# A fifth Strassen pair in two branches of a gated-mixer layer, with the weight sums made in place

## The chip, the cores and the metric

One core of a Trainium2 chip runs the whole layer. The metric is device time in microseconds (us). Names of engines as the profile has them: PE is TensorE (matmuls), PEld its weight loads, DVE is VectorE, ACT is ScalarE, POOL is GpSimd, SP is SyncE, whose queue issues most loads from HBM.

## What is computed

One layer on 256 rows of 2048 channels. An input projection `x @ w_in` gives the inputs of three mixers (a: gated linear recurrence, b: windowed attention, c: short convolution) and three gate inputs `m_a`, `m_b`, `m_c`. Each mixer's output is projected back to 2048 channels, the three are merged by sigmoid gates, projected once more, and layer-normalised. Cut to what matters here:

```python
u = x @ w_in[l]
(..., m_a, m_b, m_c) = jnp.split(u, split_idx, axis=-1)        # 2048 columns each
o_a = o_a * rsqrt(mean(o_a**2, -1) + RMS_EPS)                  # per head of 128
o_a = o_a.reshape(bsz, t, HGRN_WIDTH) * hgrn_norm_g[l]         # one weight per channel
y_a = (o_a * silu(a_g)) @ w_proj_hgrn[l]
y_b = (o_b * silu(b_g)) @ w_proj_attn[l]
y_c = (o_c * silu(c_g)) @ w_proj_conv[l]
merged = sigmoid(m_a) * y_a + sigmoid(m_b) * y_b + sigmoid(m_c) * y_c
x = layer_norm(ALPHA * x + merged @ w_out[l])
```

Everything is float32. The matmuls run on rounded operands (fp32r): each operand is split into a high part `hi` (a cast on ACT) and a low part `lo` (a subtraction on DVE), and a product is three matmuls, hi·hi + lo·hi + hi·lo.

## The kernel before

**Stages.** The time up to 526 us goes to the input projection of the mixers (functions `rows512`, `columns256`, both through `gemm`), with the mixers themselves run as generators (`hgrn`, `attn`, `sums_of_x`) that `pump()` advances a step at a time. Then come the three branches. Each branch has two halves, and a half is one *gate group* (`pair_of_groups`, which computes 1024 gate columns of `x @ w_in`) and two projections of 512 columns (`gemm(a[wp][d], outs[br], NC, "rows")`, 48 matmuls each). After the branches `gemm(a["w_out"][2], ...)`, one more `pair_of_groups` on the first 1024 columns of `w_out`, and the last 512 columns with the layer norm.

**A gate group.** Its 2048 rows of weights come as eight *pairs* of 128-row blocks, one load of 1 MB each into a `raw` buffer (pool `rawp`, three buffers). `PAIRS` says which pairs go by Strassen's scheme. An ordinary pair is two halves of 128x1024 weights: a cast to `hi` on ACT, a subtraction to `lo` on DVE, twelve matmuls, and so 24 matmuls for the pair. A Strassen pair needs seven products, 21 matmuls. Besides `hi`/`lo` of three raw blocks (128x1024 and 128x512, lines 705 to 708) it needs four sums of weights: three subtractions on DVE write them into a tile `w` (lines 702 to 704, straight from `raw`), one cast on ACT gives `hw` (128x2048), and one subtraction on DVE gives `lw` (128x2048, line 712). Before, pairs 1, 3, 5 and 7 are Strassen pairs in all seven groups, and each group opens with an ordinary pair. The matching sums of x (`sums`) are made once by `sums_of_x`; those of the merged rows (`msums`) by `turn`.

**What sets the order.** The kernel is written in order, and a scheduler interleaves the instructions when the program is built; on the chip each engine then runs its own list strictly in order. A list waits at an instruction until the tiles that it reads are written and the buffer that it writes is free. `hi` has four buffers, `lo` four, `raw` three; `hw` and `lw` are single buffers in pool `mgp`, with a second one from pool `w8` for every other Strassen pair (`spare`). A `raw` buffer is loaded again (SP's queue, line 688) once its last reader is done.

**Lines that the steps touch.** L114/L115: cast to hi, hw and subtraction to lo, lw. L702 to L704: sums of weights. L677 to L679: the matmuls of a gate group. L143 to L145: those of a projection. L191: copies of finished accumulators on ACT. L596: the norm weights of mixer a, multiplied into its gate on POOL. L766 to L769: four loads of 1 MB (x, and the layer norm's weights) issued from ACT's queue near the end.

Of the kernel before, what the change touches and what calls it, by code (L numbers as in the profile page):

```python
# [50 lines left out]
def hybrid_kernel(ctx, tc, a, out):  # L51
# [501 lines left out]
    def sums_of_x():  # L553

        n = len(pairs)
        xr = rawp.tile([P, n, 2, T], F32, tag="raw", name="xr")
        for i, p in enumerate(pairs):
            nc.sync.dma_start(out=xr[:, i], in_=a["xT"][:, 2 * p : 2 * p + 2])
        sx = t8([P, 4, n, P], "sx")
        block_sums([sx[:, j] for j in range(4)], xr[:, :, 0, :P], xr[:, :, 1, :P], xr[:, :, 0, P:], xr[:, :, 1, P:])  # L560
        yield
        for i in range(0, n, 2):
            dst = t8([P, 2, 4, 2, P], "sums", F32R)
            sums.append(dst)
            for j in range(2):
                split_to(dst[:, j], sx[:, :, i + j])
            yield
# [81 lines left out]
    msums = []  # L649

    def turn(m, d):
        dst = t8([P, 4, 2, T], "m", F32R)
# [275 lines left out]
```

## Time and profile before

| | us |
|---|---|
| median of 3 runs | 1004.09 (1003.54 to 1006.46) |
| the profiled execution | 1005.54 |
| its span, first to last instruction | 1003.6 |
| PE busy | 985.9 (98%) |
| PE weight loads busy | 833.0 (83%) |
| DVE busy | 808.5 (81%) |
| ACT busy | 562.7 (56%) |
| POOL busy | 33.0 (3%) |

The span is the stretch that the trace covers; the 1.9 us between it and the execution's own time lie around it. Busy shares are averages over the stages. What matters is whether the list of one engine ever stands still for another, and how far ahead of PE the casts and subtractions run.

### The profile page before, as it was taken

How to read it: one execution, taken by the hardware profiler on the slowest of the kernel's cores; microseconds unless marked ns; L12 is line 12 of the kernel's file. 1: busy time of each engine (PE TensorE's matmuls, PEld its weight loads, DVE VectorE, ACT ScalarE, POOL GpSimd, SP SyncE). 2: the span in 40 equal slices, each digit the busy share in tenths (PEclk: the TensorE clock that was granted, in tenths of full speed). 3: DMA queues.
4: the chain of work that ended last, by engine and by line, in shares of the span. 5: the costliest groups of instructions: out<-in, count | busy, mean ns of one | idle time of the engine just before them, and what ended most of it. 6: DMA issues, size and time to landing. Idle time of an engine off the chain costs nothing.

```text
span 1003.6 us, 13714 instructions
## 1 busy us (share of the span) xinstructions
PE 985.9 (98%) x5418; PEld 833.0 (83%) x5418; DVE 808.5 (81%) x1022; ACT 562.7 (56%) x735; POOL 33.0 (3%) x32
## 2 busy tenths in 40 slices
PE   8999999999999999999999999999999999999995
PEld 5888888888888888888888888888888888888884
DVE  6557889689965667768778898897989889897997
ACT  5545668557564655645655555555555555564551
POOL 1000100220010000000000000000000000000003
PEclk9999999999999999999999999999999999999998
DMA  8745545444455446544455655555556556548542
GB/s 315 262 172 206 173 163 171 166 171 169 169 182 196 174 162 196 182 169 166 174 200 178 220 198 206 210 205 194 216 183 210 209 195 215 180 169 336 205 167 84
DMA packets 30831, 193.67 MB, mean 193 GB/s; under 512 B 3840, under 2 KB 4640, under 8 KB 8752
## 3 DMA queue, kind: packets, MB, share of 16 engines
q1 hardware_dynamic: 28944, 185.90, 52.2%
q10 hardware_dynamic: 1152, 4.72, 1.2%
q0 software_dynamic: 672, 2.20, 0.8%
q8 instruction: 42, 0.69, 0.3%
q14 instruction: 21, 0.17, 0.0%
HBM read 190.68 MB, written 2.12 MB: 192 GB/s over the span
## 4 chain that ended last, share of the span: by engine, by line
PE 92%; DVE 5%; DMA 1%; issue 1%; ACT 1%; SPq 0%; DVEq 0%; ACTq 0%
PE acc L151 24%; PE acc L150 11%; PE acc L143 9%; PE p L677 9%; PE acc L145 9%; PE p L679 9%; PE p L678 9%; PE acc L144 9%; DVE lo L115 1%; PE acc L153 1%; PE sc L464 1%; PE pvb L507 1%; DMA raw<-in_w_rows 1%; DVE xres L799 1%; PE pT L497 1%
## 5 line engine op out<-in xcount | busy, mean ns | idle before, releaser
L114 ACT CAST hi<-raw 128x1024 fp32r<-128x1024 f32 (+1 forms) x341 | 343.9, 1013 | 320.6 <-PE p L678 107.3
L115 DVE TENSOR_TENSOR lo<-raw,hi 128x1024 fp32r<-128x1024 f32 (+1 forms) x341 | 396.9, 1175 | 107.3 <-ACT hi L114 105.5
L151 PE MATMUL acc<-xs,hi 128*128 128x512 f32 x1056 | 371.4, 396 | 0.0
L150 PE MATMUL acc<-xs,lo 128*128 128x256 f32 x990 | 278.4, 281 | 0.0
L151 PEld LDWEIGHTS acc<-xs,hi 128*128 128x128 f32 x1056 | 196.8, 188 | 43.4
L150 PEld LDWEIGHTS acc<-xs,lo 128*128 128x128 f32 x990 | 186.8, 189 | 2.4
L677 PE MATMUL p<-hi,xs 128*128 128x512 f32 x240 | 93.4, 389 | 0.0
L678 PE MATMUL p<-hi,xs 128*128 128x512 f32 x240 | 93.4, 389 | 0.0
L679 PE MATMUL p<-lo,xs 128*128 128x512 f32 x240 | 93.4, 389 | 0.0
L115 DVE TENSOR_TENSOR lw<-w,hw 128x2048 fp32r<-128x2048 f32 x28 | 64.2, 2292 | 22.2 <-ACT hw L114 20.8
L143 PE MATMUL acc<-hi,xs 128*128 128x512 f32 (+1 forms) x160 | 60.6, 379 | 2.3 <-ACT hi L114 2.3
L114 ACT CAST hw<-w 128x2048 fp32r<-128x2048 f32 x28 | 53.6, 1913 | 11.4 <-DVE w L704 11.2
L145 PE MATMUL acc<-lo,xs 128*128 128x512 f32 (+1 forms) x160 | 59.5, 374 | 0.0
L144 PE MATMUL acc<-hi,xs 128*128 128x512 f32 (+1 forms) x160 | 59.4, 371 | 0.0
L679 PEld LDWEIGHTS p<-lo,xs 128*128 128x128 f32 x240 | 45.1, 188 | 9.4
L678 PEld LDWEIGHTS p<-hi,xs 128*128 128x128 f32 x240 | 45.1, 188 | 9.3
L677 PEld LDWEIGHTS p<-hi,xs 128*128 128x128 f32 x240 | 45.0, 188 | 9.3
L191 ACT COPY rest<-acc 128x256 f32<-128x256 f32 x66 | 24.0, 372 | 42.3 <-PE acc L151 41.6
L143 PEld LDWEIGHTS acc<-hi,xs 128*128 128x128 f32 x160 | 30.4, 190 | 10.0 <-ACT hi L114 4.5
L145 PEld LDWEIGHTS acc<-lo,xs 128*128 128x128 f32 x160 | 30.4, 191 | 5.9 <-DVE lo L115 0.8
L702 DVE TENSOR_TENSOR w<-raw 128x1024 f32<-128x1024 f32 x28 | 34.2, 1221 | 1.2 <-DMA raw<-in_w_gate 0.9
L144 PEld LDWEIGHTS acc<-hi,xs 128*128 128x128 f32 x160 | 30.6, 191 | 4.9
(263 smaller groups left out, 1476.4 us busy)
## 6 DMA issues: line engine op xcount, KB each, us to landing
raw<-in_w_cols SPq DMA_DIRECT2D x68, 1024.0 KB, 4.8
raw<-in_w_gate SPq DMA_DIRECT2D x48, 1024.0 KB, 4.8
raw<-in_w_out SPq DMA_DIRECT2D x16, 1024.0 KB, 4.8
raw<-in_w_rows SPq DMA_DIRECT2D x12, 1024.0 KB, 4.8
raw<-in_w_proj_hgrn SPq DMA_DIRECT2D x8, 1024.0 KB, 4.7
raw<-in_w_proj_attn SPq DMA_DIRECT2D x8, 1024.0 KB, 4.8
raw<-in_w_proj_conv SPq DMA_DIRECT2D x8, 1024.0 KB, 4.8
raw<-in_w_rows SPq DMA_DIRECT2D x7, 512.0 KB, 9.2
```

Source lines behind the costliest of these rows:

```text
L114: nc.scalar.copy(out=hi, in_=r)
L115: nc.vector.tensor_sub(out=lo, in0=r, in1=f32(hi))
L143: nc.tensor.matmul(out=acc, lhsT=xk[:, 0, ts], rhs=hi, start=first, stop=False)
L144: nc.tensor.matmul(out=acc, lhsT=xk[:, 1, ts], rhs=hi, start=False, stop=False)
L145: nc.tensor.matmul(out=acc, lhsT=xk[:, 0, ts], rhs=lo, start=False, stop=last)
L150: nc.tensor.matmul(out=acc[:, :T], lhsT=lo, rhs=xk[:, 0], start=False, stop=False)
L151: nc.tensor.matmul(out=acc, lhsT=hi, rhs=xk, start=first, stop=last)
L191: nc.scalar.copy(out=rest[p], in_=acc[p, T:])
L677: nc.tensor.matmul(out=ps, lhsT=x[0], rhs=hi, start=begins, stop=False)
L678: nc.tensor.matmul(out=ps, lhsT=x[1], rhs=hi, start=False, stop=False)
L679: nc.tensor.matmul(out=ps, lhsT=x[0], rhs=lo, start=False, stop=last)
L702: nc.vector.tensor_sub(out=w[:, 0:2], in0=raw[:, 0:1].to_broadcast([P, 2, NC]), in1=raw[:, 1::2])
```

## The change

- `PAIRS` becomes two lists. The gate groups of branch b and c (four groups) take pairs 0, 2, 3, 5 and 7 by Strassen's scheme, five of eight. Those of branch a (two groups) and the group of `w_out2` take pairs 0, 2, 5 and 7, four of eight as before, but other ones: all seven groups now open with a Strassen pair.
- The four sums of weights are made in place, over the raw blocks, by four subtractions of 128x512, after `hi` and `lo` of the raw blocks are taken. The tile `w` goes away, and `raw` is now read until `lw` is done.
- In a group's first pair the products are taken in the order p3, p4, then the summed ones, then p1, p2. Before, p1 and p2 came first, or the summed ones.
- `lo` gets a fifth buffer.
- The sums of x are made in three steps (two pairs, two pairs, one) with buffers of their own, where one step did all four.
- The norm weights of mixer a are applied per channel after the transposition (a scaled copy on ACT and one instruction on DVE for each head) in place of the multiplication on POOL.

```diff
-PAIRS = (0, 1, 0, 1, 0, 1, 0, 1)
+PAIRS, FEWER = (0, 2, 3, 5, 7), (0, 2, 5, 7)
...
-    lop = ctx.enter_context(tc.tile_pool(name="lop", bufs=4))
+    lop = ctx.enter_context(tc.tile_pool(name="lop", bufs=5))
...
         for i, ps in transpose_pairs(..., "oaT"):
-            split_to(outs["a"][hf][:, i : i + 2], ps)
+            for j in range(2):
+                g = C["gn"][:, 4 * hf + i + j : 4 * hf + i + j + 1]
+                dst = outs["a"][hf][:, i + j]
+                nc.scalar.mul(out=dst[:, 0], in_=ps[:, j], mul=g)
+                nc.vector.scalar_tensor_tensor(out=dst[:, 1], in0=ps[:, j], scalar=g, in1=f32(dst[:, 0]),
+                                               op0=ALU.mult, op1=ALU.subtract)
...
-        nc.gpsimd.tensor_mul(out=gate, in0=gate, in1=C["gn"]...)
...
-            w = t8([P, 4, NC], "w")
-            nc.vector.tensor_sub(out=w[:, 0:2], in0=raw[:, 0:1].to_broadcast([P, 2, NC]), in1=raw[:, 1::2])
-            nc.vector.tensor_sub(out=w[:, 2], in0=raw[:, 3], in1=w[:, 0])
-            nc.vector.tensor_sub(out=w[:, 3], in0=raw[:, 2], in1=w[:, 2])
             hi, lo = split_w(flat[:, NC : 3 * NC])
             hi2 = hip.tile([P, HALF], F32R, tag="hi", name="hi")[:, :NC]
             lo2 = lop.tile([P, HALF], F32R, tag="lo", name="lo")[:, :NC]
             split_w(flat[:, 3 * NC :], hi2, lo2)
-            i = pairs.index(p)
-            hw, lw = [t8([P, 4, NC], name, F32R) if i % 2 and n < spare else
+
+            nc.vector.tensor_sub(out=raw[:, 1], in0=raw[:, 0], in1=raw[:, 1])
+            nc.vector.tensor_sub(out=raw[:, 0], in0=raw[:, 0], in1=raw[:, 3])
+            nc.vector.tensor_sub(out=raw[:, 3], in0=raw[:, 3], in1=raw[:, 1])
+            nc.vector.tensor_sub(out=raw[:, 2], in0=raw[:, 2], in1=raw[:, 3])
+            i = taken.index(p)
+            hw, lw = [t8([P, 4, NC], name, F32R) if i % 2 and n >= 2 - spare else
                       mgp.tile([P, 4, NC], F32R, tag=name, name=name) for n, name in enumerate(("hw", "lw"))]
-            split_w(w, hw, lw)
+            split_w(raw, hw, lw)
...
-            for n, y in enumerate(whole + summed + rest if raw_first or end else summed + rest[::-1] + whole):
+            for n, y in enumerate(whole + summed + rest if p else rest + summed[::-1] + whole):
```

How the lists of the engines change at three places that count. First, ACT where the first gate group starts (`rest` are the copies of the last accumulators of the input projection; before, `hi_5106` and `hi_5122` belong to ordinary pair 0, `hi_5144`, `hi_5148` and `hw_5152` to Strassen pair 1). Before:

```order
L114 CAST hi_5106<-raw_5104 128x1024
L114 CAST hi_5122<-raw_5104 128x1024
L114 CAST hi_5144<-raw_5138 128x1024
L191 COPY rest_5081<-acc_4995 128x256
L191 COPY rest_5084<-acc_4996 128x256
L114 CAST hi_5148<-raw_5138 128x512
L114 CAST hw_5152<-w_5140 128x2048
```

Now (`hi_5128`, `hi_5132` and `hw_5140` belong to Strassen pair 0, `hi_5167` and `hi_5183` to ordinary pair 1, `hi_5201` to Strassen pair 2):

```order
L114 CAST hi_5128<-raw_5126 128x1024
L114 CAST hi_5132<-raw_5126 128x512
L114 CAST hi_5167<-raw_5165 128x1024
L191 COPY rest_5103<-acc_5017 128x256
L191 COPY rest_5106<-acc_5018 128x256
L114 CAST hi_5183<-raw_5165 128x1024
L114 CAST hi_5201<-raw_5199 128x1024
L114 CAST hw_5140<-raw_5126 128x2048
```

The first cast of weight sums has moved behind two casts of 128x1024 that stand after `rest`, where one cast of 128x512 stood; and it belongs to the group's first pair now, no longer to its second.

Second, PE where the group of `w_out2` starts (acc is the projection before it). Before, the group's first 24 matmuls are those of ordinary pair 0 and read `hi_8140`, `hi_8156` and their `lo`; its beginning:

```order
L144 MATMUL acc_7963<-hi_8108,m_7982 128x512
L145 MATMUL acc_7963<-lo_8109,m_7982 128x512
L677 MATMUL p8_8137<-hi_8140,m_7750 128x512
L678 MATMUL p8_8137<-hi_8140,m_7750 128x512
L679 MATMUL p8_8137<-lo_8141,m_7750 128x512
L677 MATMUL p3_8135<-hi_8140,m_7750 128x512
```

Now:

```order
L145 MATMUL acc_8005<-lo_8151,m_8024 128x512
L681 MATMUL p3_8177<-hi_8186,msums_7800 128x512
L682 MATMUL p3_8177<-hi_8186,msums_7800 128x512
L683 MATMUL p3_8177<-lo_8187,msums_7800 128x512
L681 MATMUL p4_8178<-hw_8194,m_7792 128x512
L682 MATMUL p4_8178<-hw_8194,m_7792 128x512
L681 MATMUL p5_8176<-hw_8194,msums_7800 128x512
```

The fourth matmul of the group reads `hw` now; before it was the 25th. Eight matmuls read `hw` before the first reads `lw`. In the first gate group the list is alike, with six matmuls of the ordinary pair 1 between the three of p3 and the first on `hw`, which is so the tenth of the group.

Third, DVE in the first gate group of branch b, around one Strassen pair. Before:

```order
L702 TENSOR_TENSOR w_6137<-raw_6135 128x1024
L115 TENSOR_TENSOR lo_6104<-raw_6101,hi_6103 128x1024
L703 TENSOR_TENSOR w_6137<-raw_6135,w_6137 128x512
L704 TENSOR_TENSOR w_6137<-raw_6135,w_6137 128x512
L115 TENSOR_TENSOR lo_6120<-raw_6101,hi_6119 128x1024
L115 TENSOR_TENSOR lw_6150<-w_6137,hw_6149 128x2048
L115 TENSOR_TENSOR lo_6142<-raw_6135,hi_6141 128x1024
L115 TENSOR_TENSOR lo_6146<-raw_6135,hi_6145 128x512
```

Now:

```order
L115 TENSOR_TENSOR lo_6126<-raw_6123,hi_6125 128x1024
L115 TENSOR_TENSOR lo_6130<-raw_6123,hi_6129 128x512
L710 TENSOR_TENSOR raw_6123<-raw_6123 128x512
L711 TENSOR_TENSOR raw_6123<-raw_6123 128x512
L712 TENSOR_TENSOR raw_6123<-raw_6123 128x512
L713 TENSOR_TENSOR raw_6123<-raw_6123 128x512
L115 TENSOR_TENSOR lo_6165<-raw_6162,hi_6164 128x1024
L710 TENSOR_TENSOR raw_6162<-raw_6162 128x512
L115 TENSOR_TENSOR lw_6138<-raw_6123,hw_6137 128x2048
```

The sums of weights stood first, before any `lo` of their pair; now they stand behind both `lo`, and so behind the casts that those wait for. `raw` was free after `lo_6146`, and now is after `lw_6138`.

## Rows read from the trace of the kernel before

**Rows 1.** Page, part 1: busy us, share of the span, instructions.
```profile
PE 985.9 (98%) x5418; PEld 833.0 (83%) x5418; DVE 808.5 (81%) x1022; ACT 562.7 (56%) x735; POOL 33.0 (3%) x32
```

**Rows 2.** Stretches: length, busy PE, PEld, DVE, ACT, POOL (instructions), clock, DMA, GB/s.
```profile
651.03:691.83 40.80, 40.80 (x181) 33.78 (x180) 34.31 (x34) 21.45 (x21) 0.00 (x0) 1.00 0.56 199
691.83:713.60 21.77, 21.77 (x98) 18.02 (x97) 18.57 (x21) 11.33 (x11) 0.00 (x0) 1.00 0.56 203
904.00:921.00 17.00, 17.00 (x80) 14.04 (x79) 11.34 (x17) 7.03 (x9) 0.00 (x0) 1.00 1.02 415
```

**Rows 3.** Waits of PE over the span: us in total, times, longest.
```profile
PE acc L143 <- ACT hi L114: 2.3, 3, 1.7
...
PE pT L497 <- DVE s L488: 1.3, 1, 1.3
PE acc L145 <- DVE l L115: 0.8, 1, 0.8
PE p L679 <- DVE lw L115: 0.4, 1, 0.4
```

**Rows 4.** Timeline of PE: start us, us, line, operation, out<-in.
```profile
525.76 0.39 PE L677 MATMUL p<-hi,xs 128*128 128x512 f32 x1
...
531.20 0.39 PE L677 MATMUL p<-hw,sums 128*128 128x512 f32 x1
...
651.03 0.39 PE L677 MATMUL p<-hi,xs 128*128 128x512 f32 x1
...
661.23 0.39 PE L677 MATMUL p<-hi,xs 128*128 128x512 f32 x1
...
678.68 0.39 PE L679 MATMUL p<-lw,sums 128*128 128x512 f32 x1
...
926.97 0.39 PE L677 MATMUL p<-hi,m 128*128 128x512 f32 x1
```

**Rows 5.** Timeline of DVE, one Strassen and one ordinary pair of branch b.
```profile
663.87 1.23 DVE L702 TENSOR_TENSOR w<-raw 128x1024 f32<-128x1024 f32 x1 [0.40 <-DMA raw<-in_w_gate]
665.12 0.69 DVE L703 TENSOR_TENSOR w<-raw,w 128x512 f32<-128x512 f32 x1
665.73 1.22 DVE L115 TENSOR_TENSOR lo<-raw,hi 128x1024 fp32r<-128x1024 f32 x1
666.87 0.68 DVE L704 TENSOR_TENSOR w<-raw,w 128x512 f32<-128x512 f32 x1
667.73 1.23 DVE L115 TENSOR_TENSOR lo<-raw,hi 128x1024 fp32r<-128x1024 f32 x1 [0.18 <-ACT hi L114]
669.54 2.29 DVE L115 TENSOR_TENSOR lw<-w,hw 128x2048 fp32r<-128x2048 f32 x1 [0.59 <-ACT hw L114]
671.75 1.82 DVE L115 TENSOR_TENSOR lo<-raw,hi 128x1024 fp32r<-128x1024 f32 x2
```

**Rows 6.** Timeline of ACT at the first gate group and at `w_out2`.
```profile
525.61 0.79 ACT L191 COPY rest<-acc 128x256 f32<-128x256 f32 x2 [1.38 <-PE acc L151]
526.29 0.62 ACT L114 CAST hi<-raw 128x512 fp32r<-128x512 f32 x1
526.81 1.92 ACT L114 CAST hw<-w 128x2048 fp32r<-128x2048 f32 x1
...
921.59 2.00 ACT L114 CAST hi<-raw 128x1024 fp32r<-128x1024 f32 x2 [3.33 <-DMA raw<-in_w_out]
```

**Rows 7.** SP's queue: issue of the first weights of `w_out2`.
```profile
913.60 0.33 SPq L688 DMA_DIRECT2D raw<-in_w_out  x1
```

**Rows 8.** That load, issue to landing, us.
```profile
DMA to landing us min/median/max: 7.9/7.9/7.9
```

**Rows 9.** View of the DMA issues: loads, KB each, median us from issue to landing.
```profile
raw<-in_w_gate SPq DMA_DIRECT2D x48, 1024.0 KB, 4.8
...
lbt<-in_ln_b ACTq DMA_DIRECT2D x1, 1024.0 KB, 12.4
```

More of the change, by code (lines that the diff above doesn't have):

```diff
@@ L215, in constants @@
         nc.vector.tensor_copy(out=c["mask"], in_=mask)
-        c["gn"] = const.tile([P, HW], F32, name="gn")
-        nc.sync.dma_start(out=c["gn"], in_=a["hgrn_norm_g"].partition_broadcast(P))
+        c["gn"] = const.tile([P, 8], F32, name="gn")
+        nc.sync.dma_start(out=c["gn"], in_=a["hgrn_norm_g"])
         c["cw"] = const.tile([P, 8, 3], F32, name="cw")
@@ L553, in sums_of_x @@
     def sums_of_x():
[L555 to L566, printed above, removed]
+        for at in range(0, len(PAIRS), 2):
+            n = len(PAIRS[at : at + 2])
+            xr = rawp.tile([P, n, 2, T], F32, tag="raw", name="xr")
+            for i, p in enumerate(PAIRS[at : at + 2]):
+                nc.sync.dma_start(out=xr[:, i], in_=a["xT"][:, 2 * p : 2 * p + 2])
+            sx = t4([P, 4, n, P], "sx")
+            block_sums([sx[:, j] for j in range(4)], xr[:, :, 0, :P], xr[:, :, 1, :P], xr[:, :, 0, P:], xr[:, :, 1, P:])
+            yield
+            dst = t8([P, n, 4, 2, P], "sums", F32R)
+            for i, p in enumerate(PAIRS[at : at + 2]):
+                sums[p] = dst[:, i]
+                split_to(dst[:, i], sx[:, :, i])
             yield
@@ L636, in hybrid_kernel @@
         tasks.append(attn(hf, q, kz, vb, gate))
-    pairs = [p for p in range(KT // 2) if PAIRS[p]]
-    sums = []
+    sums = {}
     tasks.append(sums_of_x())
@@ L647, in hybrid_kernel @@
     ms = []
-    msums = []
+    msums, dsts = {}, []
     def turn(m, d):
@@ L662, in turn, with pair_of_groups @@
                 block_sums([sx[:, j] for j in range(4)], raw[:, 0, :P], raw[:, 1, :P], raw[:, 0, P:], raw[:, 1, P:])
-                split_to(msums[d // 2][:, d % 2], sx)
+                split_to(msums[p], sx)
             yield
-    def pair_of_groups(src, x, sums, raw_first, spare):
+    def pair_of_groups(src, x, sums, taken, spare):
         p1, p2, p6, p7 = [accp.tile([P, NC], F32, tag="acc", name=f"p{i}") for i in (1, 2, 6, 7)]
@@ L684, in pair_of_groups @@
         last = KT // 2 - 1
-        final = max(p for p in range(KT // 2) if not PAIRS[p])
+        final = max(p for p in range(KT // 2) if p not in taken)
         for p in range(KT // 2):
@@ L689, in pair_of_groups @@
             flat = raw.rearrange("p s n -> p (s n)")
-            if not PAIRS[p]:
+            if p not in taken:
                 for s in range(2):
@@ L708, in pair_of_groups @@
             split_w(flat[:, 3 * NC :], hi2, lo2)
-            i = pairs.index(p)
-            hw, lw = [t8([P, 4, NC], name, F32R) if i % 2 and n < spare else
+            nc.vector.tensor_sub(out=raw[:, 1], in0=raw[:, 0], in1=raw[:, 1])
[4 more added lines that the diff above has]
+            hw, lw = [t8([P, 4, NC], name, F32R) if i % 2 and n >= 2 - spare else
                       mgp.tile([P, 4, NC], F32R, tag=name, name=name) for n, name in enumerate(("hw", "lw"))]
-            split_w(w, hw, lw)
-            sx = [[sums[i // 2][:, i % 2, j, m] for m in range(2)] for j in range(4)]
+            split_w(raw, hw, lw)
+            sx = [[sums[p][:, j, m] for m in range(2)] for j in range(4)]
             k = 2 * p
@@ L744, in hybrid_kernel @@
         for half in range(2):
-            sg = pair_of_groups(a["w_gate"][2 * n + half], xs, sums, n > 0, 2 if n else 1)
+            sg = pair_of_groups(a["w_gate"][2 * n + half], xs, sums, PAIRS if n else FEWER, 2 if n else 1)
             for y in sg:
@@ L804, in hybrid_kernel @@
         residual(t, slice(2 * NC, 3 * NC), acc[t])
-    y = pair_of_groups(a["w_out2"][0], ms, msums, False, 0)
+    y = pair_of_groups(a["w_out2"][0], ms, msums, FEWER, 0)
     for n in range(2):
```

18 lines of the change are left out of this document (9 added, 9 removed).

## The prediction

> **What bounds the kernel now.** I read the busy shares first: PE is busy for 98% of the span, DVE for 81%, ACT for 56% [rows 1]. Then, because shares are averages, the stage that the change touches: in the stretch of one gate group PE is busy throughout, DVE for 34.3 of 40.8 us, and in the two projections behind it DVE for 18.6 of 21.8 us [rows 2]. So PE bounds both, and DVE has 6.5 and 3.2 us to spare. The granted clock is 1.00 there, the 2.4 GHz level, before and after. PE's waits say the same: over the span they are some microseconds at the start (L143), 1.3 us for an attention softmax, 0.8 us at the end, and 0.4 us for one `lw` in the first gate group [rows 3]. The price of a matmul is read from two starts in the timeline of PE: from 651.03 to 661.23 us lie 24 matmuls of an ordinary pair and 21 of a Strassen pair, 10.20/45 = 0.2267 us each [rows 4]; 180 of them make the 40.8 us of the group. That is the unit for everything below, not the duration of 0.39 us, since matmuls overlap.
>
> How far is DVE ahead? One `lw` begins at 669.54 and lasts 2.29 us, so it is done at 671.83 [rows 5]; PE first reads it at 678.68 [rows 4]. The lead is 6.9 us, and it is what must absorb anything that DVE does longer or later.
>
> **The change part by part.** The sum is made against the profiled execution, with its span of 1003.6 us and its own 1005.5 us, which is 1.45 us above the median of the runs. I carry the difference over to the median.
>
> *Fewer matmuls.* Four groups have one more Strassen pair, each three matmuls less: 12 x 0.2267 = 2.7 us gained, all on PE, which sets the end.
>
> *The first gate group.* It opens with a Strassen pair now, so `hw` is needed nine matmuls after its start, 2.04 us, where it was needed after 24 (525.76 to 531.20 [rows 4]). ACT's list there is: two `rest`, which wait for the last accumulators of the projection and began 0.15 us before the group; two casts of 128x1024; then `hw`. From rows: `rest` 0.68 us from start to next start, `hw` 1.92 us, and two casts of 128x1024 in 2.00 us, so 0.96 each when another follows [rows 6]. 0.68 + 0.96 + 0.96 + 1.92 = 4.52, less 0.15, is 4.4 us after the start. PE stands still for 4.4 - 2.0 = 2.3 us, in one wait or in several for what lies on the way. Bounds: 1.4 if one of the casts is done early, 3.3 if another is caught before it. I take +2.3.
>
> *The weight sums in place.* From the starts on DVE [rows 5], a Strassen pair costs today: sums 1.25 + 0.61 + 0.60, `lo` 1.14 and 0.60, `lw` 2.21, together 6.4 us; an ordinary pair two `lo`, 2.3 us. Now there are four sums of 128x512. Each reads what the instruction before it wrote or overwrites what it read; such a step starts 1.25 us behind a 128x1024 subtraction, where an independent one starts 1.14 behind (663.87 to 665.12 against 665.73 to 666.87). That is 0.11 more, so up to 4 x 0.71 = 2.8 us of sums, and 6.8 us for a pair. In the groups of four pairs DVE does 4 x 0.4 = 1.6 us more, 35.9 of 40.8: not a bound. In a group of five it does 34.3 + 4 x 0.4 + (6.8 - 2.3) = 40.4 us, while PE now needs 177 x 0.2267 = 40.1. Its spare time is gone. On top come its waits for `hw`, 0.59 us in a pair today, which grow if anything: ACT can't begin the cast until the sums behind both `lo` are done, and DVE has one `lo` to do meanwhile. Five of them are 3.0 us, so DVE falls 0.3 + 3.0 = 3.3 us behind in a group, and the two projections give back just 3.2. The lead of 6.9 covers most of it; but the sums can't run ahead as before, since they stand behind the casts, and `raw`, with three buffers, is free only after `lw`, with 4.8 us to load the next [rows 9]. The group's last pair has its `hw` only after that whole chain. Bounds for a group: 0 (the lead covers it) and 3.3 (none of it does). I take 1.0, nearer to the low end because the lead is twice the deficit: 4 x 1.0 = +4.0, from 0 to 13.2. Who waits is PE, for `hw` or `lw` late in a group or for the first `lo` of the projection behind it. The other two groups (branch a): the 0.4 us that PE waits for `lw` today [rows 3] once more, +0.4.
>
> *The group of `w_out2`.* Its first weights are issued at 913.60 and take 7.9 us [rows 7, 8], to 921.5, as four loads from ACT's queue are under way; the group starts at 926.97 [rows 4]. From landing to `hw` there is now one chain: cast 1.05, `lo` 1.25, sum 0.60, `lo` 0.60, three sums 0.72 + 0.72 + 0.69, `hw` 1.92, 7.55 us in all, to 929.05. PE wants `hw` after three matmuls, at 927.65: it waits 1.4 us. Then eight matmuls on `hw` cover 1.81 of the 2.29 us of `lw`: 0.5 more. +1.9. Bounds: a load of 4.8 us gives nothing to wait for, one of 12.4 us [rows 9] 6.4.
>
> There the Trainium skill (DMA: Bandwidth & Descriptors, Queues, rings and completion order) says that each DMA engine takes turns between the queues that it has work for, packet by packet. By that rule the load shares with ACT's queue: half of 415 GB/s [rows 2] would be 5.05 us for 1.05 MB in place of 2.5, so 7.3 us for the load, and the term 1.3 in place of 1.9. The 7.9 us of the row is more than that, and I keep the row.
>
> *The end.* The last 512 columns wait 0.8 us for DVE's `l` today [rows 3]. DVE enters them from a group with heavier sums: once more +0.8, bounds 0 and 1.6.
>
> *At nothing.* The norm weights (POOL's two multiplications go, ACT and DVE get eight short instructions each) and the sums of x in three steps lie in the projection of the mixers, where no wait in rows 3 but that of 1.3 us stands. That one lies in the stretch of the sums of x, and smaller steps may remove it: -1.3 at best, 0 taken. If their cover is missing, PE waits for an instruction of about 0.7 us: +0.7. The fifth `lo` buffer costs nothing.
>
> Sum: -2.7 + 2.3 + 4.0 + 0.4 + 1.9 + 0.8 = +6.7 us. Span 1010.3, execution 1012.2, on the scale of the median 1010.8.
>
> **The rivals.** *The lead holds, and it is no slower.* DVE is 6.9 us ahead, `lo` has one buffer more, and five sums of 3.3 us of deficit are given back in each pair of projections. Then the groups cost nothing and only the starts do: if ACT's casts at the first group and the load of `w_out2` come early as well, -2.7 + 1.4 = -1.3, 1002.8; with the softmax wait gone too, 1001.5, and with no wait at the first group 1000.1. It decides where `hw` is ready before PE's tenth matmul. For it: the lead in the rows. Against: ACT's list at the first group, which has 4.5 us of work behind `rest`, and can't start earlier.
>
> *The starts cost, the groups don't.* -2.7 + 2.3 + 0.4 + 1.9 + 0.8 = +2.7: 1006.8, no difference to speak of. It decides at a deficit below the lead in each group.
>
> *DVE becomes the bound.* No lead is kept, since `raw` is held until `lw`: each group costs 3.3. -2.7 + 2.3 + 13.2 + 0.4 + 1.9 + 0.8 = +15.9: 1020. For it: 40.4 against 40.1 us before any wait. Against: the projections give 3.2 back.
>
> That the change doesn't do what it says I leave out: the order of the matmuls shows the shorter groups.
>
> **How the numbers follow.** 0.3%, about what a measurement of this kernel can tell from no change, is 3 us. The forecast (1007 to 1015) has 0.56, the starts alone (1003 to 1008) 0.22, DVE as the bound 0.12, and the lead that holds 0.10. The range of 1003 to 1018 leaves out most of the last and the upper part of the bound. Faster by over 0.3% is half of the case in which the lead holds, 0.05; within 0.3% are its other half and most of the case of the starts alone, 0.20; slower are the forecast, the bound and the rest, 0.75.
>
> **What would show it.** Right: twelve matmuls fewer than the 5418 of rows 1; PE waiting for `hw` L114 some 2 us at the first gate group and at `w_out2`; in the stretch of a five-pair group DVE busy for 39 us or more of 40 to 42, and waits of PE below 2 us near its end. Wrong: a five-pair group of 40.1 us with DVE below 38 (the lead holds); PE waiting at every pair (the bound); or a lower granted clock after one of the waits, which no term has.

## The result, and the profile after

The changed kernel takes 1014.57 us (median of 4, 1012.95 to 1015.51) against 1004.18 us (1003.54 to 1006.46): a ratio of 1.0099, interval 1.0087 to 1.011, so 10.4 us slower. The prediction was 1010.8 us, in a range of 1003 to 1018. The direction was right. The sum was too small by 3.2 us in the profiled execution (span 1013.5, 9.9 us more than before), and that is a net figure: five places cost 5.1 us more than their terms, and a term of 1.9 us came to nothing.

Part 1 of the page, which answers to [rows 1] (busy us, share of the span, instructions):

```profile
PE 991.7 (98%) x5406; PEld 830.1 (82%) x5406; DVE 830.4 (82%) x1083; ACT 566.3 (56%) x744; POOL 25.7 (3%) x30
```

The twelve matmuls are gone. The other lines of interest are the waits of PE (us in total, times, longest), to be read against [rows 3]:

```profile
PE acc L143 <- ACT hi L114: 2.5, 2, 2.3
PE p L681 <- ACT hw L114: 2.3, 4, 0.9
PE acc L145 <- DVE l L115: 2.1, 1, 2.1
...
PE p L683 <- DVE lo L115: 0.6, 1, 0.6
PE acc L143 <- DVE sg L732: 0.6, 1, 0.6
PE acc L145 <- DVE lo L115: 0.4, 1, 0.4
PE p L683 <- DVE lw L115: 0.2, 1, 0.2
```

`hw` and `lo` have come in, which [rows 3] don't have; `l` has gone from 0.8 to 2.1 us; the wait of 1.3 us for a softmax is gone. These waits sum to less than the loss, so I cut the span at the first matmul of each gate group and compare stretch by stretch. In the view of stretches (length, busy PE, PEld, DVE, ACT, POOL with instructions, granted clock, DMA share, GB/s), from one group's start to the next:

```profile
525.93:592.97 67.04, 65.42 (x277) 52.59 (x276) 54.12 (x58) 34.63 (x34) 0.00 (x0) 0.97 0.51 189
592.97:656.42 63.45, 63.29 (x278) 51.53 (x276) 55.33 (x59) 34.04 (x34) 0.00 (x0) 1.00 0.52 199
656.42:719.27 62.85, 62.57 (x274) 50.84 (x273) 58.09 (x64) 34.30 (x33) 0.00 (x0) 1.00 0.56 201
719.27:783.11 63.84, 62.89 (x274) 50.74 (x273) 60.73 (x68) 35.86 (x35) 0.00 (x0) 1.00 0.53 198
783.11:846.23 63.12, 62.62 (x275) 50.78 (x274) 59.04 (x66) 33.75 (x33) 0.00 (x0) 1.00 0.54 200
846.23:935.41 89.18, 88.55 (x402) 71.82 (x401) 81.15 (x106) 49.77 (x57) 0.00 (x0) 1.00 0.62 236
935.41:1001.65 66.24, 64.11 (x324) 53.89 (x323) 59.09 (x76) 29.32 (x32) 4.43 (x4) 1.00 0.39 148
```

I call them a1, a2 (branch a), b1, b2, c1, c2 (with the projection to the first columns of the output) and the end (group of `w_out2` and last columns). The kernel before has 62.71, 62.56, 62.56, 62.56, 62.56, 88.26 and 64.88 for them. So a1 lost 4.33 us, a2 0.89; b1 to c2 lost 0.29 + 1.28 + 0.56 + 0.92 = 3.05, although they have 2.72 us of matmuls less: 5.8 us of waiting; the end lost 1.36. With 0.17 before the first group and 0.06 behind the last matmul, 9.9 us.

a1 has a second thing to see: its granted clock is 0.97. Timeline of PE there (start, us, line, operation, out<-in, idle time ahead and releaser):

```profile
526.61 0.39 PE L681 MATMUL p<-hi,xs 128*128 128x512 f32 x1
...
528.93 0.50 PE L683 MATMUL p<-lo,xs 128*128 128x512 f32 x1 [0.64 <-DVE lo L115]
530.30 0.50 PE L681 MATMUL p<-hw,xs 128*128 128x512 f32 x1 [0.87 <-ACT hw L114]
...
531.75 0.63 PE L682 MATMUL p<-hw,sums 128*128 128x512 f32 x1
532.18 0.63 PE L681 MATMUL p<-hw,sums 128*128 128x512 f32 x1
...
536.13 0.39 PE L681 MATMUL p<-hi,xs 128*128 128x512 f32 x1
```

The tenth matmul starts at 530.30, 4.37 us after the group, where nine matmuls take 2.04: 2.33 us of waiting. Then the matmuls stand 0.43 us apart in place of 0.227. The granted clock is at half, which is 1.2 GHz, for 3.4 us. That costs 1.5 us more: from the matmul at 530.30 to the next group's start it is 62.67 us here, and 61.16 in e2 below, which has the same pairs in branch a and no fall of the clock there.

```profile
531.30:534.70 3.40, 3.40 (x9) 2.62 (x8) 2.24 (x2) 0.00 (x0) 0.00 (x0) 0.50 0.76 248
```

The fall is not certain: with the same two idle times of 0.64 and 0.87 or 0.88 us in this place the clock fell here, in e7 and in e11, and did not in e2. Of the clock's rise at a kernel's start the Trainium skill (TensorE: Matmul & The Clock Gate, Part 1: The HAM clock gate) says that it comes after a different number of matmuls from run to run. That is said of the rise; of the fall, these runs show the like.

### The profile page after: what moved, and what is told of

It reads as the page before. It is cut to its first block, busy times and chain, and to the rows that moved or that the text cites. A ratio compares the mean times of both kernels' runs of the same rounds, so it can differ in the third digit from the quotient of the medians.

```text
span 1013.5 us, 13677 instructions
## 1 busy us (share of the span) xinstructions
PE 991.7 (98%) x5406; PEld 830.1 (82%) x5406; DVE 830.4 (82%) x1083; ACT 566.3 (56%) x744; POOL 25.7 (3%) x30
## 4 chain that ended last, share of the span: by engine, by line
PE 88%; DVE 7%; DMA 2%; ACT 2%; issue 1%; SPq 0%; ACTq 0%
PE acc L151 24%; PE acc L150 12%; PE acc L145 9%; PE acc L143 8%; PE acc L144 8%; PE p L681 7%; PE p L683 7%; PE p L682 7%; DVE lo L115 2%; ACT hi L114 1%; DMA raw<-in_w_gate 1%; ACT hw L114 1%; DVE lw L115 1%; PE sc L469 1%; PE pvb L512 1%; PE acc L153 1%
## 5 line engine op out<-in xcount | busy, mean ns | idle before, releaser
L114 ACT CAST hi<-raw 128x1024 fp32r<-128x1024 f32 (+1 forms) x341 | 340.3, 1007 | 325.2 <-PE p L682 90.3
L681 PE MATMUL p<-hi,xs 128*128 128x512 f32 x216 | 84.8, 392 | 0.1
L683 PE MATMUL p<-lo,xs 128*128 128x512 f32 x216 | 84.2, 392 | 0.7 <-DVE lo L115 0.6
L682 PE MATMUL p<-hi,xs 128*128 128x512 f32 x216 | 84.4, 391 | 0.0
L115 DVE TENSOR_TENSOR lw<-raw,hw 128x2048 fp32r<-128x2048 f32 x32 | 73.3, 2291 | 12.1 <-ACT hw L114 12.1
L114 ACT CAST hw<-raw 128x2048 fp32r<-128x2048 f32 x32 | 61.0, 1908 | 10.8 <-DVE raw L713 10.8
L683 PEld LDWEIGHTS p<-lo,xs 128*128 128x128 f32 x216 | 40.7, 188 | 10.1 <-DVE lo L115 1.5
L681 PEld LDWEIGHTS p<-hi,xs 128*128 128x128 f32 x216 | 40.9, 189 | 9.0 <-ACT hi L114 0.5
L682 PEld LDWEIGHTS p<-hi,xs 128*128 128x128 f32 x216 | 40.7, 189 | 8.6
L681 PE MATMUL p<-hw,sums 128*128 128x512 f32 x84 | 33.9, 403 | 1.4 <-ACT hw L114 1.4
```

The lines of the kernel that those rows point to most:

```text
L114: nc.scalar.copy(out=hi, in_=r)
L115: nc.vector.tensor_sub(out=lo, in0=r, in1=f32(hi))
L681: nc.tensor.matmul(out=ps, lhsT=x[0], rhs=hi, start=begins, stop=False)
L682: nc.tensor.matmul(out=ps, lhsT=x[1], rhs=hi, start=False, stop=False)
L683: nc.tensor.matmul(out=ps, lhsT=x[0], rhs=lo, start=False, stop=last)
```

## The experiments

All times are medians, all ratios against the kernel before on the same chip. Stretches are worked out from the starts of the groups, as above; "half clock" is the time after the first 30 us, up to the last matmul, at which the granted clock was at 0.5 in the profiled execution. Each stretch comes from one execution. The changed kernel and e7, whose lists of instructions are the same up to the end, differ by 0.1 us in a1 and a2 and by 2.1 us from b1 to c2, so in kernels with sums in place a smaller difference there says little; the stretches without waits (62.56 us) repeat to 0.01 us.

| | sums | pairs (b, c) | pairs (a, `w_out2`) | us | ratio, interval | a1 | a2 | b1 to c2 | end | half clock |
|---|---|---|---|---|---|---|---|---|---|---|
| before | apart | 1 3 5 7 | 1 3 5 7 | 1004.2 | 1 | 62.71 | 62.56 | 275.94 | 64.88 | 0 |
| after | in place | 0 2 3 5 7 | 0 2 5 7 | 1014.57 | 1.0099 (1.0087-1.0110) | 67.04 | 63.45 | 278.99 | 66.24 | 3.4 |
| e1 | in place | 0 2 3 5 7 | 2 3 5 7 | 1015.65 | 1.0097 (1.0081-1.0112) | 64.43 | 63.52 | 279.04 | 69.22 | 3.4 |
| e2 | in place | 0 2 5 7 | 0 2 5 7 | 1017.16 | 1.0112 (1.0099-1.0126) | 65.53 | 63.49 | 280.12 | 67.99 | 3.4 |
| e3 | in place | 1 3 4 5 7 | 1 3 5 7 | 1016.79 | 1.0109 (1.0095-1.0122) | 64.06 | 62.82 | 277.39 | 73.87 | 6.8 |
| e4 | apart | 1 3 4 5 7 | 1 3 5 7 | 1008.58 | 1.0026 (1.0016-1.0037) | 63.02 | 62.56 | 275.65 | 69.23 | 6.8 |
| e5 | in place | 1 3 5 7 | 1 3 5 7 | 1015.41 | 1.0102 (1.0088-1.0115) | 63.90 | 62.83 | 280.23 | 69.73 | 3.4 |
| e6 | apart | 1 3 5 7 | 1 3 5 7 | 1009.61 | 1.0039 (1.0028-1.0050) | 62.56 | 62.56 | 275.97 | 69.91 | 6.8 |
| e7 | as after, end reordered | | | 1013.67 | 1.0089 (1.0075-1.0102) | 67.10 | 63.50 | 281.12 | 63.90 | 3.4 |
| e8 | as e4, end reordered | | | 1002.70 | 0.9978 (0.9968-0.9987) | 62.96 | 62.56 | 275.45 | 63.55 | 0 |
| e9 | as e6, raw held | | | 1012.31 | 1.0061 (1.0046-1.0077) | 63.07 | 63.06 | 278.01 | 70.11 | 6.8 |
| e10 | as e6, end reordered | | | 1002.56 | 0.9971 (0.9960-0.9983) | 62.56 | 62.56 | 276.02 | 64.44 | 0 |
| e11 | as e8, pairs as after | | | 1016.47 | 1.0113 (1.0100-1.0127) | 66.63 | 62.56 | 286.36 | 63.07 | 13.7 |
| e12 | as e5, five `hi`, four `lo` | | | 1013.30 | 1.0087 (1.0070-1.0104) | 64.33 | 62.96 | 280.14 | 67.61 | 3.4 |

**e1: only branch a and `w_out2` open with ordinary pairs.**

```diff
-PAIRS, FEWER = (0, 2, 3, 5, 7), (0, 2, 5, 7)
+PAIRS, FEWER = (0, 2, 3, 5, 7), (2, 3, 5, 7)
```

> The changed kernel with one difference: the lists of four Strassen pairs (both groups of branch a and the group of w_out2) are 2, 3, 5 and 7, so these groups open with two ordinary pairs. Branches b and c keep 0, 2, 3, 5, 7. If the opening Strassen pair is what makes the first gate group 4.3 us longer (2.3 us until hw comes, the rest while the clock is at half), that group falls from 45.3 us to about 41.0, the half clock at its start is gone in every run, and the second group of branch a falls from 41.7 to about 41.0: 5.0 us in all, 1014.6 to about 1009.6. If the late casts of ACT at the end of the input projection delay the group whichever pair opens it, the first group stays above 44 us and the time at 1013 to 1015.

Half a hit. The wait and the half clock at the start of a1 are gone, but a1 is only 2.6 us shorter, not 4.3: it keeps 1.7 us over the kernel before, and a2 1.0. The end has grown by 3.0, since PE now waits 3.3 us for `l` and the half clock has moved there. No gain in all. So the opening pair causes the wait at the start of a1, and something else costs in groups that open with an ordinary pair (0.95 us of it is one wait for `hw` in a1, at 557.85).

**e2: no fifth pair.**

```diff
-PAIRS, FEWER = (0, 2, 3, 5, 7), (0, 2, 5, 7)
+PAIRS, FEWER = (0, 2, 5, 7), (0, 2, 5, 7)
```

> The changed kernel with four Strassen pairs (0, 2, 5, 7) in every group, so without the fifth pair; 12 matmuls more, 2.7 us. If DVE's volume in a group of five pairs is what PE waits for (5.8 us of waits in four groups, by the lengths of the stretches), these waits go nearly all and the time is 1014.6 - 5.8 + 2.7 = 1011.5, with DVE at some 36 us of 40.8 in a group. If the lateness comes from where the sums stand in a pair (behind both lo, hw after them), four pairs wait as well at the last pair of each group, and the time is 1014.6 + 2.7 - 1 = 1016 or more.

The time has not fallen to 1011.5, and with four pairs too b1 to c2 hold 280.12 - 275.94 = 4.2 us of waiting. So DVE's volume in a group of five, on which my term rested, is not what PE waits for in the main; the 1.6 us that the fifth pair adds to it is within the spread between executions. The second reading holds.

**e3, e4: every group opens with an ordinary pair, with the sums in place and apart.** e3:

```diff
-PAIRS, FEWER = (0, 2, 3, 5, 7), (0, 2, 5, 7)
+PAIRS, FEWER = (1, 3, 4, 5, 7), (1, 3, 5, 7)
```

and e4 besides makes the sums as before, ahead of `hi` and `lo`, into a tile `w` (and gives up the second `hw`/`lw`, `spare` 0, for the room):

```diff
+            w = t8([P, 4, NC], "w")
+            nc.vector.tensor_sub(out=w[:, 0:2], in0=raw[:, 0:1].to_broadcast([P, 2, NC]), in1=raw[:, 1::2])
+            nc.vector.tensor_sub(out=w[:, 2], in0=raw[:, 3], in1=w[:, 0])
+            nc.vector.tensor_sub(out=w[:, 3], in0=raw[:, 2], in1=w[:, 2])
             hi, lo = split_w(flat[:, NC : 3 * NC])
...
-            nc.vector.tensor_sub(out=raw[:, 1], in0=raw[:, 0], in1=raw[:, 1])
...
-            split_w(raw, hw, lw)
+            split_w(w, hw, lw)
```

> The changed kernel with other lists: five pairs 1, 3, 4, 5, 7 and four pairs 1, 3, 5, 7. Every group opens with an ordinary pair; the weight sums are still made in place, the number of matmuls is that of the changed kernel. If DVE's volume is the cause in branches b and c (40.4 us of work for 40.1 us of PE), it is the same here, their waits stay near 5.8 us, and only the 5.0 us of branch a go: 1009.5. If the lead of DVE at a group's beginning is the cause (a Strassen pair that opens a group is asked for at once, when DVE still owes the group before), most of the 5.8 us goes too: 1004 to 1006. Groups of five pairs then take 40.1 to 40.6 us.

> As the run before (pairs 1, 3, 4, 5, 7 and 1, 3, 5, 7), but with the weight sums made as in the kernel before: first of all in a pair, straight from raw, by one subtraction of 128x1024 and two of 128x512 into a tile of their own, raw free before lw; no second buffer for hw and lw, since the tile takes its room. DVE's work in a group of five is 34.3 + 4.1 = 38.4 us of 40.1. If the sums' place in the pair (behind both lo) and raw's long hold are what makes hw late, no group waits and the whole gain of 2.7 us shows: 1004.2 - 2.7 + 0.5 = 1002. If a fifth pair costs its gain in any form, since DVE has under 2 us to spare in a group: 1005 to 1008.

e3's time is a miss for both theories. b1 to c2 keep 4.2 us of waiting (277.39 - 275.94 + 2.72), as many as e5 below has with four pairs (4.3), and its end is the longest of all: 2.5 us for `hw` in the first Strassen pair of `w_out2`, 3.3 us for `l`, and half clock behind each. In e4 the groups are clean: a2 as before, b1 to c2 0.3 us shorter than before. Its time is lost at the end alone, 4.35 us, where PE waits 3.2 us for `l` and has 6.8 us of half clock behind it.

**e5, e6: the sums alone.** Four pairs 1, 3, 5, 7 in every group, sums in place (e5) and apart as in e4 (e6).

> The changed kernel with the pairs of the kernel before (1, 3, 5, 7) in every group: the sums of weights in place are all that is left of the change in the groups. If the sums in place are a cause by themselves (they stand behind both lo, and raw is held until lw), groups of four pairs wait too: 63.2 us or more from one group's start to the next in branches b and c where the kernel before has 62.56, and PE waits 3 us or more for l near the end: 1013 to 1017. If only the fifth pair and the opening pair cost, the groups are back at 62.6 and the time at 1005 to 1007.

> As the run before, but with the sums of weights made first of all, straight from raw, into a tile of their own, and no second buffer for hw and lw. What is left of the change: norm weights per channel, sums of x in steps, a fifth lo buffer, and the order of the products in a group's first pair, which is not a Strassen pair here. If the sums in place are the cause, the groups take 62.6 us again in branches b and c; the first gate group starts at 524.2 to 525.9 us; near the end PE waits some 3 us for l, since the tile of the sums takes the room of the last h, and the time is 1007 to 1009, or 1005 if the clock doesn't fall after that wait. If the groups stay above 63 us, something else in the change slows them: 1010 or more.

This pair decides between sums in place and sums apart. In e6 every stretch from a1 to c1 is 62.56 us, the time of 276 matmuls at 0.2267, without a wait; in e5 a1 is 63.90, b2 63.92 and c1 64.00, while a2 and b1 lose only 0.2 to 0.3 us. The whole difference of the two kernels, 5.8 us, is that of a1 to c2 (406.96 against 401.09). The pairs and the matmuls are the same. What differs is the place of the sums, with the hold of `raw` that goes with it, and one subtraction more on DVE in each pair; the second `hw` buffer, which e5 has and e6 hasn't, would speak the other way. The volume on DVE is not the cause: in b2 DVE is busy for 57.1 us in e5, and for 60.0 in e8 below, whose b2 takes 62.41 us.

Timelines of the last pair of b2, first e5 (the group starts at 714.61), ACT, then DVE, then PE:

```profile
743.43 1.57 ACT L114 CAST hi<-raw 128x1024 fp32r<-128x1024 f32 x2
748.32 1.06 ACT L114 CAST hi<-raw 128x1024 fp32r<-128x1024 f32 x1 [3.32 <-PE p L682]
750.99 1.05 ACT L114 CAST hi<-raw 128x1024 fp32r<-128x1024 f32 x1 [1.62 <-PE p L682]
751.95 1.91 ACT L114 CAST hw<-raw 128x2048 fp32r<-128x2048 f32 x1
...
743.57 2.29 DVE L115 TENSOR_TENSOR lw<-raw,hw 128x2048 fp32r<-128x2048 f32 x1 [0.59 <-ACT hw L114]
745.77 1.82 DVE L115 TENSOR_TENSOR lo<-raw,hi 128x1024 fp32r<-128x1024 f32 x2
747.51 0.69 DVE L710 TENSOR_TENSOR raw<-raw 128x512 f32<-128x512 f32 x1
...
749.57 1.22 DVE L115 TENSOR_TENSOR lo<-raw,hi 128x1024 fp32r<-128x1024 f32 x1
750.70 0.68 DVE L713 TENSOR_TENSOR raw<-raw 128x512 f32<-128x512 f32 x1
...
753.91 0.50 PE L681 MATMUL p<-hw,sums 128*128 128x512 f32 x1 [0.69 <-ACT hw L114]
```

and e6 (starts at 713.09):

```profile
742.98 0.62 ACT L114 CAST hi<-raw 128x512 fp32r<-128x512 f32 x1 [0.67 <-PE p L682]
744.73 1.92 ACT L114 CAST hw<-w 128x2048 fp32r<-128x2048 f32 x1 [1.12 <-DVE w L708]
746.54 1.05 ACT L114 CAST hi<-raw 128x1024 fp32r<-128x1024 f32 x1
```

`hw` begins (751.95 and 744.73) 37.3 us into the group in e5 and 31.6 in e6. In e6 the sums need `raw` alone, and `hw` follows the pair's own casts. In e5 the pair's own casts (743.43, one of 128x1024 and one of 128x512) wait for nothing, but the sums come behind the `lw` of the pair before and both `lo`, from 747.51 on. In ACT's list the casts of the next weights, those of the projection behind the group, now stand ahead of `hw` (748.32 and 750.99). Each of them waits for one of the four `hi` buffers, which PE frees ("<-PE p L682", 3.32 and 1.62 us), and `hw` begins as the second ends, although the sums are done at 751.38. It is done at 753.86, and PE has stood for it. So `hw` can't run ahead of PE: in e5 it is done 0.8 to 1.2 us ahead of PE's first read of it in a2 and b1, and 0.1 us ahead in b2, c1 and c2; in e6 3.8 to 9.4 us in all of these. No run moved `hw` alone in ACT's list, so how the loss divides between that order and the late sums is open.

**e7: the end reordered.** The residual sums and statistics of the first 1024 columns are written behind the `l` of the last 512 columns.

```diff
-    for n in range(2):
-        for t in range(2):
-            residual(t, slice(n * NC, n * NC + NC), y[n][:, t])
...
                 parts.append(split_w(raw[:, s], h8[:, s], l8[:, s]))
+    for n in range(2):
+        for t in range(2):
+            residual(t, slice(n * NC, n * NC + NC), y[n][:, t])
```

> The changed kernel with one difference at the end: the sums of the residual and their statistics (some 6 us of DVE) are written behind the l of the last 512 columns, not ahead of the last two of them. If DVE's list is what keeps the last columns waiting, PE's wait of 2.1 us for l goes, and with it any fall of the clock there; what was moved ends later but before the last matmuls: 1014.6 - 2.1 = 1012.5. If the wait only moves (the accumulators or the layer norm come later), the time stays at 1014 to 1015.

The wait for `l` is gone and the end is 2.3 us shorter, so it was the residual sums ahead of `l` in DVE's list that kept the last columns waiting. Only 1.0 us shows in the ratio: in this execution b2, c1 and c2 are 0.6 to 0.9 us longer than in the changed kernel's, with the same list of instructions up to there. I take it that with sums in place a group feels when each load lands (ACT waits 19.2 us for landings of gate weights in the changed kernel, never in e6); that wasn't tested by itself.

**e8, e10: versions that beat both.** e8 is e4 with the end of e7, and with the last `h` in room that the merged rows have left; e10 is the same with four pairs.

```diff
-                    h8, l8 = t8([P, 2, HALF], "h8", F32R), t8([P, 2, HALF], "l8", F32R)
-                parts.append(split_w(raw[:, s], h8[:, s], l8[:, s]))
+                    l8 = t8([P, 2, HALF], "l8", F32R)
+                h8 = mgp.tile([P, HALF], F32R, tag="merged", name="h8", bufs=4)
+                parts.append(split_w(raw[:, s], h8, l8[:, s]))
```

> Sums of weights apart, pairs 1, 3, 4, 5, 7 and 1, 3, 5, 7, as in the earlier run of five pairs, with two differences at the end: the last h take room that the merged rows have left, so they no longer wait for the lw that reads the tile of sums, and the residual sums stand behind l. If the end is what cost that version its gain (PE's wait of 3.2 us for l and 6.8 us at half the clock behind it), the wait and the half clock go: the stretch from the start of the last group to the last matmul falls from 69.2 to about 64.3 us, and the time from 1008.6 to about 1003.5, 0.2% under the kernel before. If PE waits elsewhere instead or the half clock stays, 1006 or more.

> The fastest version so far (sums apart, ordinary opening, reordered end) with four pairs 1, 3, 5, 7 in every group: the fifth pair by itself, on a base without waits in the groups. If the fifth pair is worth its 12 matmuls less the small waits that the trace shows in such a group (62.40 to 62.56 us in place of 62.56), it is worth 0.4 us: 1003.1 against 1002.7. If it is worth its whole 2.7 us, 1005.4.

1002.70 and 1002.56 us: both are faster than the kernel before, by 0.2 to 0.3%, and there is no half clock left. Little of that is Strassen's: of the 3.2 us by which e8's span is shorter, 1.1 lie before the first group, 1.3 in the end, 0.5 behind the last matmul and 0.2 in the branches; of e10's 2.5 us 0.1 lies in the branches. Which of e8's two edits at the end removed the wait for `l` was not separated. The fifth pair is worth nothing that can be measured in the time (the two intervals overlap), against 0.4 and 2.7 us in the two readings; from b1 to c2 it shortens e8 by 0.6 us against e10, and a1 is 0.4 us longer. A clean group of five in e8:

```profile
712.67:775.08 62.41, 62.40 (x275) 51.02 (x274) 59.99 (x63) 36.27 (x35) 0.00 (x0) 1.00 0.57 203
```

62.41 us where 273 matmuls are 61.89, with no gap of PE long enough for the view of waits. Two neighbouring Strassen pairs are unavoidable with five of eight, and with single buffers the second one's `hw` is cast only when PE has read the first: ACT's row for the second of them, c1 of e8, waits for PE.

```profile
799.85 1.91 ACT L114 CAST hw<-w 128x2048 fp32r<-128x2048 f32 x1 [0.54 <-PE p L682]
```

**e9: raw held, sums early.** e6 with one short instruction behind each `lw` that reads `raw`.

```diff
             split_w(w, hw, lw)
+            held = sm.tile([P, 1], F32, name="held")
+            nc.vector.tensor_sub(out=held, in0=f32(lw[:, 3, NC - 1 :]), in1=raw[:, 0, :1])
```

> The version with the sums apart and four pairs (1, 3, 5, 7), with one thing put back: a subtraction of 128x1 behind each lw reads raw, so that raw is held until lw is done, as it is when the sums are made in place; the sums themselves still stand first in the pair. It adds 28 short instructions on DVE and leaves out nothing. If the long hold of raw (the next load starts late) is what makes the groups with sums in place 63.9 us long in branches b and c, the groups go from 62.56 to 63 us or more and the time to 1013 or more. If the place of the sums behind both lo is the cause, the groups stay at 62.6 us and the time at 1008 to 1011.

Inconclusive by length, clear by waits. Every stretch is 0.5 us longer, but PE waits nowhere in the groups of branches a to c, and ACT never for a landing of gate weights. The matmuls themselves stand further apart: 0.232 us for 26 of them in each Strassen pair (some 24 us of a group), beginning with the first that reads `hw`, and 0.2267 for the others. So the hold alone makes no wait while the sums are early; where the 0.5 us come from is open.

**e11: opening pairs with the sums apart.** e8 with the lists of the changed kernel.

> The fastest version so far with the lists of the changed kernel (0, 2, 3, 5, 7 and 0, 2, 5, 7), so that every group opens with a Strassen pair while the sums are made early, apart from raw. If the opening pair costs because ACT has casts to do between the last copies of the input projection and hw, wherever the sums stand, the first gate group is 2.3 us longer at least (65.3 us or more to the next group, 67 where the clock falls), other openings cost up to 3 us where the tile of sums has to wait for room, and the time is 1006 to 1011. If only sums in place make an opening pair late, 1002 to 1004.

The time is a miss, over the highest that was expected. a1 is 66.63, with the same idle times of PE at its start as in the changed kernel: the first opening costs the same wherever the sums are made, since ACT's list is what delays it. The openings of a2, b2 and c1 cost nothing (62.56, 62.25, 61.99), those of b1 and `w_out2` 4.5 and 7 us, half clock included. PE, then DVE:

```profile
658.82 0.50 PE L681 MATMUL p<-hw,xs 128*128 128x512 f32 x1 [2.03 <-ACT hw L114]
...
927.00 0.80 PE L145 MATMUL acc<-lo,m 128*128 128x512 f32 x1 [4.36 <-DVE lo L115]
...
923.39 1.22 DVE L706 TENSOR_TENSOR w<-raw 128x1024 f32<-128x1024 f32 x1 [8.92 <-DMA raw<-in_w_out]
```

The last two rows: DVE's list has the first sum of `w_out2` ahead of `lo` of the projection before it, and stands 8.9 us for a load. A sum made early in the list makes everything behind it wait when its load is late.

**e12: a fifth buffer for `hi`** in e5, against one of `lo`.

```diff
-    hip = ctx.enter_context(tc.tile_pool(name="hip", bufs=4))
+    hip = ctx.enter_context(tc.tile_pool(name="hip", bufs=5))
...
-    lop = ctx.enter_context(tc.tile_pool(name="lop", bufs=5))
+    lop = ctx.enter_context(tc.tile_pool(name="lop", bufs=4))
```

> The version with the sums in place and four pairs 1, 3, 5, 7, with five buffers for hi in place of four, and four for lo in place of five (the room is the same). Theory: sums in place can't run ahead of PE, since they stand behind lo, lo behind the cast hi, and hi waits for a buffer that PE's matmuls of an earlier pair must have read; hw of a pair is so tied to PE's own progress. One more hi buffer lets the chain start some 11 matmuls, 2.5 us, earlier: PE's waits for hw at the last pair (0.85 us in each group of branches b and c) go, the groups fall from 63.9 us to 62.6 to 63.0, and the time from 1015.4 to about 1011. Rival: the chain itself (DVE's time, or raw held until lw) makes hw late; then the buffer changes nothing, 63.7 us or more and 1014 to 1016.

PE's waits for `hw` are gone, as the theory has it, but b1 to c2 are as long as in e5 (280.14 against 280.23), with waits for `lw`. What ACT waits for, e5 and then e12 (us in total, times, longest), and ACT at the last pair of b2 in e12:

```profile
ACT hi L114 <- PE p L682: 103.9, 51, 3.4
ACT hi L114 <- DMA raw<-in_w_gate: 12.8, 4, 4.7
```

```profile
ACT hi L114 <- DMA raw<-in_w_gate: 59.8, 13, 6.5
ACT hi L114 <- PE p L682: 26.6, 21, 5.3
...
749.33 1.05 ACT L114 CAST hi<-raw 128x1024 fp32r<-128x1024 f32 x1 [4.79 <-DMA raw<-in_w_proj_attn]
750.38 1.92 ACT L114 CAST hw<-raw 128x2048 fp32r<-128x2048 f32 x1
```

The buffer took away most of the wait for PE, and the landing of `raw` took its place. `hw` stands behind a cast of the next weights here too, and these land late: with sums in place a `raw` buffer is free only after `lw`, which ended at 744.44, and SP issued their load at 744.47. The sums themselves are done at 750.35, no sooner than that cast. Two ties hold the chain, and loosening one shows the other. The gain in time (1.0102 to 1.0087; the intervals overlap) lies in the end, where the wait for `l` was 2.1 us in place of 3.3.

## Why the prediction came out as it did

- **Fewer matmuls, -2.7.** Right: 5406, and where nothing waits most of it shows: 0.57 of a group's 0.68 us in c1 of e11.
- **The first gate group, +2.3.** The wait was 2.33 us, by the steps given: `rest` at 525.77, two casts, `hw` from 528.35 to 530.25. The stretch lost 4.33. The rest is 1.5 us of half clock and 0.5 of smaller gaps, which e2 has too (65.53, so 2.82 lost without a fall of the clock). "A lower granted clock after one of the waits, which no term has" is what failed here: an idle PE has a second price.
- **Four groups of five pairs, +4.0.** Measured 5.8, each 1.0 to 2.0. The step that failed is "The lead of 6.9 covers most of it". I set DVE's deficit against a lead that I took for a stock, and the reason that the same sentence gives against it (the sums can't run ahead as before) did not enter the figure. The lead was misread too: 6.9 us is that of one pair in b1, and in b2 and c1 of the same trace `lw` of the second and third Strassen pairs is done 3.1 us ahead of PE's read, less than the deficit of 3.3. DVE and PE at the second pair of b2 in the kernel before:

```profile
725.67 2.29 DVE L115 TENSOR_TENSOR lw<-w,hw 128x2048 fp32r<-128x2048 f32 x1 [1.24 <-ACT hw L114]
...
731.04 0.39 PE L679 MATMUL p<-lw,sums 128*128 128x512 f32 x1
```

  And a lead of `lw` existed because sums needed `raw` alone. In place they need `hi` and both `lo`, and `hw` comes behind casts that wait for PE, so the lead is gone with four pairs as with five (e2, e5 against e6). The volume wasn't the cause (e8 has as much, without the waits), and it was forecast too high: DVE's busy time in b1, b2 and c1 grew by 5.2, 4.4 and 4.9 us (58.1, 60.7 and 59.0 against 52.9, 56.3 and 54.1) where the sum has 6.1, and in b1's group it is 36.2 of 40.2 us, not the 39 or more that would have shown the forecast right:

```profile
656.42:696.60 40.18, 39.90 (x175) 32.06 (x174) 36.20 (x37) 22.55 (x22) 0.00 (x0) 1.00 0.52 183
```

  That 4.0 lies near 5.8 is luck of the middle value.
- **The other group of branch a, +0.4.** 0.89, and the same cause: e11, with the same pairs and the sums apart, has it at 0.
- **`w_out2`, +1.9.** Nothing: its group took 41.55 us to the first matmul of the last columns, before 41.47. SP issued its first load at 918.36, 17.0 us ahead of the group, where I kept the 13.4 of before (913.60 to 926.97 [rows 4, 7]):

```profile
918.36 22.28 SPq L692 DMA_DIRECT2D raw<-in_w_out  x5
```

  The load itself took longer than the 7.9 us that I kept, 9.2, and `hw` was done at 935.57, half a microsecond ahead of PE's need at 936.09. The term was one of distance, and the distance moved. Nor were the 7.9 us a price of sharing: in the trace before, this load moved its first packet at 915.7 us, 2.1 us after its issue, and ACT's queue its last at 915.9, so the two hardly overlapped, and why the load took 7.9 us is open. In the changed kernel they do overlap. ACT's queue has the DMA engines alone until 921.8, when the load moves its first packet, 3.4 us after its issue (1.0 us in quiet stretches). From then on each queue has half. The queues from 918.4 to 921.8 us, then from 922 to 931 us (packets, MB, share of the DMA engines' time):

```profile
q10 hardware_dynamic: 195, 1.43, 100.4%
q1 hardware_dynamic: 1, 0.01, 0.6%
...
q1 hardware_dynamic: 252, 1.93, 50.8%
q10 hardware_dynamic: 258, 1.92, 50.4%
```

  The second stretch is as the rule of turns packet by packet has it (the Trainium skill, DMA: Bandwidth & Descriptors, Queues, rings and completion order); the first is not.

- **The end, +0.8.** PE waited 2.1 us for `l` in place of 0.8, 1.3 more. Named rightly, 0.5 too small: the residual sums stand ahead of `l` in DVE's list, and the wait goes when they are moved behind it (e7).
- **At nothing.** The softmax wait went. The first gate group started at 524.2 to 525.9 us in the thirteen profiled executions of changed kernels, before at 525.76: between -1.6 and +0.2, not isolated. In e10 it is 1.6 of the 2.5 us by which the span is shorter.

Of the rivals, "DVE becomes the bound" is refuted by the 5.8 us of waiting in place of its 13.2, and by e2; and "the lead holds" and "the starts cost, the groups don't" by the 5.8 us from b1 to c2.

## What to carry to other kernels

A lead is not a stock that a deficit eats into; ask which buffers and readers tie the producer to the consumer, since making something in place puts it behind every reader of what it overwrites, and look at what then stands ahead of it in each engine's list. Read a lead in several groups, not in one. Price a wait of the matmul engine with the clock that may fall with it: 1.4 to 2.9 us here, behind waits of 2.0 to 4.4 us and behind two short ones. And saving matmuls takes cover from the casts and sums beside them: the fifth Strassen pair was worth nothing measurable even on the best version.

## What the runs showed of the hardware

- The granted clock fell to half during PE's waits or shortly behind them, from 1.3 us before a wait's end (e11) to 1.4 us behind it (e3). With single waits of 2.5 to 4.4 us it did so in each of the profiled executions (e1, e3, e4, e5, e6, e9, e11), for 3.4 us or for 6.8; with one of 2.1 us in e2 and e12 and not in the changed kernel; with one of 2.0 us that had one of 0.8 ahead of it in e11; with 0.84 us (before) not at all. Its price, read from the same 102 matmuls behind the wait for `l`, which take 15.89 us before and in the changed kernel: 17.3 to 17.5 us with 3.4 us of half clock (e1, e2, e3, e5, e12), so 1.4 to 1.6 us; 18.6 to 18.7 with 6.8 us (e4, e6, e9), so 2.7 to 2.9. A stretch of e6 around the end of its wait of 3.2 us:

```profile
976.80:983.60 6.80, 5.93 (x16) 4.87 (x17) 6.80 (x8) 0.00 (x0) 0.00 (x0) 0.52 0.01 4
```

- Matmuls can stand 2% further apart (0.232 in place of 0.2267 us) with no wait in the records and the clock at 1.00 (e9); the cause is open.
- Two queues with work shared the DMA engines' time in halves (50.8% and 50.4%, 922 to 931 us of the changed kernel), but a load that was issued while the other queue was busy moved its first packet only 3.4 us after its issue.
